# Pinned places for joins, weight loads, transposes and modulation pieces, and another prologue, in a hybrid DeltaNet and RWKV-7 block

## The chip, the core and the metric

The kernel runs on one core of a Trainium2 chip. The metric is the device time of one execution in microseconds (us); lower is better. The engines are TensorE (PE, with its weight loads shown apart as PEld), VectorE (DVE), ScalarE (ACT), GpSimd (POOL) and SyncE (SP), which here only issues DMAs. Each engine works through its own instructions in a fixed order; it waits where an operand or a buffer isn't ready, and everything behind the waiting instruction waits too.

## What is computed

One decoder block on 512 tokens of width 1024, in float32. A conditioning vector `c` gives six vectors of modulation; two token mixers run beside each other on one input projection and are merged by gates; a gated convolutional feed-forward follows.

```python
cond = jax.nn.silu(c)
mod = cond @ w_ada[i] + b_ada[i]
shift1, scale1, gate1, shift2, scale2, gate2 = jnp.split(mod[:, None, :], 6, axis=-1)
h = rms_norm(x, norm1_w[i]) * (1.0 + scale1) + shift1
p = h @ w_in[i]
qkv_a, z_a, b_a, a_a, p_b, gl_a, gl_b = split_cols(p, IN_SIZES)
y_a = gated_deltanet(qkv_a, z_a, b_a, a_a, conv_gdn[i], a_log[i], dt_bias[i], onorm_gdn[i])
y_b = rwkv7_time_mix(p_b, mu_rwkv[i], w0[i], w2[i], a0[i], a2[i], g2[i], k_k[i], k_a[i], ...)
merged = sigmoid(gl_a) * (y_a @ w_branch_gdn[i]) + sigmoid(gl_b) * (y_b @ w_branch_rwkv[i])
x = x + gate1 * (merged @ w_out[i])
h = rms_norm(x, norm2_w[i]) * (1.0 + scale2) + shift2
x = x + gate2 * conv_glu(h, w_ffn_in[i], conv_ffn[i], w_ffn_out[i])
return rms_norm(x, norm_f_w)
```

Both mixers have 8 heads of width 64 and are computed in chunks of 64 tokens. In each chunk a unit lower triangular 64x64 matrix is inverted for each head (the reference's `triangular_solve`, and its counterpart for RWKV-7).

## The kernel before

**Layout and products.** Channels lie on the 128 partitions and the 512 tokens along the free axis. A product is one output tile of 128 channels: for each of 8 blocks of 128 inputs `mm3` issues three matmuls (high part of the weight by high part of the input, high by low, low by high: L186, L189, L190), which together give float32 accuracy. One full product is 24 matmuls of 128x128x512. `weights` brings a weight tile: SP loads it into `raw` (two buffers, 512 KB), ACT casts it to `whi` (L145), DVE forms the difference `wlo` (L148).

**Queue of products.** Products wait in the list `queue`; the generator `stream` issues them a triple at a time, `fill(n)` takes n triples, `need(label)` runs until a product is done, `insert` puts products in front. `weights` is called for the product now running and the next one. So the rest of the program is written between calls of `fill`, which mix products with the mixers' small matmuls. A scheduler then gives every engine its order; an edge of the class `after` ("place") only orders two instructions of one engine and makes nothing wait.

**Order of the stages.** In the prologue the square sum of `x` is taken over channels (squares on ACT, L352, adds on DVE, L354, a matmul by ones, L356). `c` arrives broadcast to 128 partitions; its SiLU is the first work of ACT (L94). `first_tiles` then computes seven products at once, block by block (`first_h`: modulation of a block, then its normalized input `hh`, `hl`). The remaining products of the input projection stand in this order: queries of the delta rule, two low-rank tiles (LO1, LO2), `z` (Z0 to Z3, stored to DRAM in `zsc`), delta-rule values (GV0 to GV3), RWKV keys and receptances (RK, RR), values (RV), gates of the first branch (GA0 to GA7), between which the eight branch products `bg` are inserted, and gates of the second (GB). Then come branch (`br`), output (`o`) and feed-forward (`fi`, `fo`) products, from about 490 us to the end.

**Solve and joins.** `solve` inverts 32x32 diagonal blocks. It stores them to DRAM (`lsc`, four DMAs, L560), loads them regrouped by block into `lt` (L563), transposes and masks (`ti`, DVE L564, POOL L565), and makes 30 pairs of DVE steps of growing width (L571, L573). After its `yield` the joins combine the blocks: four groups of 32 tiny matmuls (L594, L604), with a copy on ACT (L599) between two groups. It runs once for the delta rule (`g`), and once for RWKV-7 (`r`).

**Modulation pieces.** 32 column blocks of `w_ada`, each in two halves, make 64 pieces. `ada_half` loads a piece (`wada`, one buffer, 256 KB) and reduces it against `cond` on DVE (L209). They are attached to products by `late`.

**Transposes.** `to_natural` turns a tensor from channels to tokens in four blocks: four transposes on PE (L616) and four copies out of PSUM (L619) each. It is applied to `rv_`, `bh` and `kh`, after the `bg` products.

Of the kernel before, what the change touches and what calls it, by code (L numbers as in the profile page):

```python
# [55 lines left out]
def body(ctx, tc, io, out, tap=lambda name, ap: None):  # L56
# [121 lines left out]
    last = {"step": None, "hold": False, "gate": None, "norm": None}  # L178
# [4 lines left out]
    def mm3(p, w, j, x, start, stop):  # L183
        hi, lo = (a[j] for a in w)
        xh, xl = x
        i = pe.matmul(p, hi, xh, start=start, stop=False)  # L186
        if last["hold"]:
            tc.add_manual_dep(i.ins, last["step"].ins.name, after, reason="place")
        pe.matmul(p, hi, xl, start=False, stop=False)  # L189
        pe.matmul(p, lo, xh, start=False, stop=stop)  # L190
        return i
# [13 lines left out]
    def ada_half(j, u):  # L205
        w = wp.tile([128, T], F32, name="wada", tag="wada")
        part = slice(T * u, T * u + T)
        sp.dma_start(w, io["w_ada"][j][:, part])
        i = dve.tensor_tensor_reduce(out=w, in0=w, in1=cond[:, part], scale=1.0,  # L209
                                 scalar=half[:, j:j + 1] if u else col("b_ada", j), op0=ALU.mult, op1=ALU.add,  # L210
                                 accum_out=(mod if u else half)[:, j:j + 1])
        if last["gate"] is not None:
            tc.add_manual_dep(i.ins, last["gate"].ins.name, after, reason="place")
            last["gate"] = None

    first_half = []
# [13 lines left out]
    def stream():  # L230
        while queue:
# [113 lines left out]

    table(SILU)
    fn(cond, cond, AF.Silu)
    table(EXP)
    total = tmp("rs")
    for k in range(KT):  # L350
        sq = total if k == 0 else tmp("sq")
        act.activation(sq, xT(k), AF.Square)  # L352
# [3 lines left out]
    pe.matmul(p, one, total, start=True, stop=True)  # L356
# [4 lines left out]
    first_ps = [mm(), mm(), pa(), pa(), pc(), pc(), pc()]  # L361
# [4 lines left out]
    first_w = []  # L366

    def load_ada(k):
        for j in ((0,), (1, 2))[k] if k < 2 else (k + 1,):
            if j < KT:  # L370
                w = slot((2, 3, 8, 9, 12)[j]) if j < 5 else slot2((0, 2, 1)[j - 5])
                first_w.append(w)
                sp.dma_start(w[:, 0:D], io["w_ada"][8 + j])
                sp.dma_start(w[:, D:2 * D], io["w_ada"][j])

    def first_h(k):
# [110 lines left out]
    last["gate"] = dve.scalar_tensor_tensor(gl, s3, -1.0, bc(nea), op0=ALU.mult, op1=ALU.mult)  # L487
# [65 lines left out]
    def solve(sv, name, work):  # L553
# [9 lines left out]
        sp.dma_start(lt, lsc)  # L563
# [22 lines left out]
        yield  # L586
        for h in range(2):
# [636 lines left out]
```

## Time and profile before

| | |
|---|---|
| median of 3 runs | 934.77 us (933.60 to 935.44) |
| profiled execution | 937.31 us |
| its span, first to last instruction | 935.6 us |
| mean granted TensorE clock | 0.983 |
| modulation pieces, DVE (L209) | 64 reductions, first at 91.9 us, last at 480.4 us |
| solve `g`: stores of `lsc` issued, first step, joins | 121.5, 143.1, about 205 to 212 us |
| solve `r`: stores of `lsc` issued, load of `lt` issued | 314.3, 328.9 us |
| transposes of `rv_`, `bh`, `kh` on PE | up to 381 us |

The profile is one execution; idle time stands in square brackets in front of an instruction, with what ended it. The granted clock is TensorE's, 1 for full speed.

### The profile page before, as it was taken

The numbers are of one execution on the slowest core, as the hardware profiler recorded it, in microseconds if no ns is written. First come the engines' busy times: TensorE is split into PE (matmuls) and PEld (weight loads), VectorE is DVE, ScalarE is ACT, GpSimd is POOL, SyncE is SP. The second block draws the span as 40 slices with busy tenths as digits, with TensorE's granted clock in tenths as the row PEclk, the third lists the DMA queues.
The fourth block names the chain that finished last, engine by engine and source line by source line (L and its number), as shares of the span: only waits on it lengthen the run. The fifth ranks groups of instructions, "written<-read, shape, count | busy, mean of one in ns | idle before, by whom it ended". The sixth has DMA issues, their size and how long they took to land.

```text
span 935.6 us, 13853 instructions
## 1 busy us (share of the span) xinstructions
PE 876.3 (94%) x5459; PEld 687.7 (74%) x5459; DVE 533.3 (57%) x858; ACT 419.2 (45%) x680; POOL 95.2 (10%) x91
## 2 busy tenths in 40 slices
PE   2999999999989978899999999999999999999996
PEld 1886577677656666677668888888888888888885
DVE  5987859824696786255476537564445445332233
ACT  5367543734554747632465335343333333333231
POOL 1000300000352300001230120000000000010112
PEclk9999999997999989899999999999999999999998
DMA  9841245363323367644546542322322322533322
GB/s 332 283 149 67 91 105 185 109 166 112 103 82 113 69 213 267 162 147 148 183 158 202 171 141 84 111 91 92 109 92 90 105 99 90 179 98 100 107 80 91
DMA packets 81119, 125.72 MB, mean 134 GB/s; under 512 B 26045, under 2 KB 42813, under 8 KB 80990
## 3 DMA queue, kind: packets, MB, share of 16 engines
q1 hardware_dynamic: 81054, 124.83, 42.2%
q8 instruction: 43, 0.70, 0.3%
q14 instruction: 22, 0.18, 0.1%
HBM read 110.13 MB, written 14.16 MB: 133 GB/s over the span
## 4 chain that ended last, share of the span: by engine, by line
PE 69%; DVE 10%; DMA 6%; ACT 6%; issue 6%; POOL 2%; SPq 0%; DVEq 0%; POOLq 0%; ACTq 0%
PE ps_mm L186 19%; PE ps_mm L189 18%; PE ps_mm L190 18%; DMA wada<-in_w_ada 4%; DVE wlo L148 2%; PE ps_pc L181 2%; DVE wada L209 1%; ACT tmp_rs L94 1%; PE ps_pc L186 1%; PE ps_pc L189 1%; PE ps_pc L190 1%; ACT slot L619 1%; PE ps_pa L186 1%; PE ps_pa L189 1%; PE ps_pa L190 1%
## 5 line engine op out<-in xcount | busy, mean ns | idle before, releaser
L186 PE MATMUL ps_mm<-hh,whi 128*128 128x512 f32 (+1 forms) x642 | 264.2, 412 | 9.8 <-ACT hh L308 3.4
L148 DVE TENSOR_TENSOR wlo<-raw,whi 128x1024 fp32r<-128x1024 f32 (+2 forms) x140 | 161.2, 1152 | 176.2 <-ACT whi L145 170.6
L190 PE MATMUL ps_mm<-hh,wlo 128*128 128x512 f32 (+1 forms) x642 | 255.0, 399 | 1.3 <-DVE wlo L148 1.3
L189 PE MATMUL ps_mm<-hl,whi 128*128 128x512 f32 (+1 forms) x642 | 253.8, 396 | 0.0
L145 ACT CAST whi<-raw 128x1024 fp32r<-128x1024 f32 (+2 forms) x140 | 137.1, 979 | 259.7 <-PE ps_mm L189 198.4
L186 PEld LDWEIGHTS ps_mm<-hh,whi 128*128 128x128 f32 x642 | 121.5, 190 | 46.8 <-issue 8.5
L190 PEld LDWEIGHTS ps_mm<-hh,wlo 128*128 128x128 f32 x642 | 121.6, 189 | 31.6 <-issue 3.4
L189 PEld LDWEIGHTS ps_mm<-hl,whi 128*128 128x128 f32 x642 | 122.1, 190 | 26.7 <-issue 4.0
L186 PE MATMUL ps_mm<-slot,whi 128*128 128x512 f32 (+1 forms) x226 | 85.7, 379 | 4.7 <-ACT tmp_sp L94 4.7
L190 PE MATMUL ps_mm<-slot,wlo 128*128 128x512 f32 (+1 forms) x226 | 85.1, 376 | 0.0
L189 PE MATMUL ps_mm<-slotd,whi 128*128 128x512 f32 (+1 forms) x168 | 62.4, 371 | 0.0
L186 PEld LDWEIGHTS ps_mm<-slot,whi 128*128 128x128 f32 x226 | 43.2, 191 | 12.6 <-ACT tmp_sp L94 4.9
L190 PEld LDWEIGHTS ps_mm<-slot,wlo 128*128 128x128 f32 x226 | 43.1, 191 | 7.7
L189 PE MATMUL ps_mm<-slot,whi 128*128 128x512 f32 (+1 forms) x122 | 45.3, 372 | 0.0
L186 PE MATMUL ps_mm<-slotd,whi 128*128 128x512 f32 (+1 forms) x96 | 36.4, 379 | 0.0
L190 PE MATMUL ps_mm<-slotd,wlo 128*128 128x512 f32 (+1 forms) x96 | 36.1, 376 | 0.0
L209 DVE CUSTOM_DVE_ANT_0 wada<-wada,cond,cols 128x512 f32<-128x512 f32 x32 | 25.6, 800 | 18.3 <-DMA wada<-in_w_ada 18.2
L189 PEld LDWEIGHTS ps_mm<-slotd,whi 128*128 128x128 f32 x168 | 31.6, 188 | 5.7
L1099 DVE TENSOR_TENSOR tmp_sg<-tmp_acc,ps_mm 128x512 f32<-128x512 f32 x20 | 13.8, 688 | 36.0 <-PE ps_mm L190 35.8
L209 DVE CUSTOM_DVE_ANT_0 wada<-wada,cond,half 128x512 f32<-128x512 f32 x32 | 24.9, 779 | 14.6 <-DMA wada<-in_w_ada 14.4
L398 DVE SCALAR_TENSOR_TENSOR tmp_acc<-ps_mm,cols,tmp_acc 128x511 f32<-128x511 f32 (+2 forms) x44 | 32.8, 746 | 0.7
L1032 POOL COPY tmp_rs<-tmp_sq 128x512 f32<-128x512 f32 x2 | 2.1, 1064 | 304.0 <-ACT tmp_sq L1029 304.0
(270 smaller groups left out, 1262.5 us busy)
## 6 DMA issues: line engine op xcount, KB each, us to landing
raw<-in_w_in SPq DMA_DIRECT2D x40, 512.0 KB, 4.1
raw<-in_w_fi SPq DMA_DIRECT2D x37, 512.0 KB, 3.5
wada<-in_w_ada SPq DMA_DIRECT2D x64, 256.0 KB, 2.7
raw<-in_w_fo SPq DMA_DIRECT2D x16, 512.0 KB, 3.6
slot<-in_w_ada SPq DMA_DIRECT2D x10, 512.0 KB, 8.5
slot<-in_xT SPq DMA_DIRECT2D x16, 256.0 KB, 4.6
raw<-in_w_out SPq DMA_DIRECT2D x8, 512.0 KB, 3.4
raw<-in_w_in SPq DMA_DIRECT2D x8, 448.0 KB, 4.5
```

The source lines that it names most:

```text
L94: i = act.activation(*a, **k)
L145: i = act.copy(hi, src)
L148: j = eng.tensor_tensor(lo, src, hi.bitcast(F32), op=ALU.subtract)
L181: last["step"] = pe.matmul(*a, **k)
L186: i = pe.matmul(p, hi, xh, start=start, stop=False)
L189: pe.matmul(p, hi, xl, start=False, stop=False)
L190: pe.matmul(p, lo, xh, start=False, stop=stop)
L209: i = dve.tensor_tensor_reduce(out=w, in0=w, in1=cond[:, part], scale=1.0, scalar=half[:, j:j + 1] if u else col("b_ada", j), op0=ALU.mult ...
L398: dve.scalar_tensor_tensor(acc[:, i:], p[:, :T - i], w[:, taps - 1 - i:taps - i], acc[:, i:], op0=ALU.mult, op1=ALU.add)
L619: (act.copy if e == c or quiet else dve.tensor_copy)(place(e, 2 * b + c), p[hs(c), :, e, :])
L1032: pool.tensor_copy(sums[0], sq)
L1099: dve.tensor_tensor(t, accs[j], p, op=ALU.mult)
```

## The change

The computation and its results stay the same; only places and one layout change.

Prologue: `c` comes as one row (4 KB in two loads), is broadcast by a matmul with ones into PSUM, and SiLU reads it there, behind the sixth square. `cols` and the first half of the first modulation weights are loaded between tiles of `x`. 34 small matmuls by ones are added on PE ahead of and behind the sum matmul. The first scale `A1` is made on DVE.

```diff
-        if k == 3:
-            sp.dma_start(cond, io["c"])
-    sp.dma_start(cols, io["cols"])
+        if k == 2:
+            sp.dma_start(cols, io["cols"])
+        if k == KT - 2:
+            sp.dma_start(first_w[0][:, 0:D], io["w_ada"][8])
...
-    fn(cond, cond, AF.Silu)
-    table(EXP)
+    i = work(8, None)
+    for u in range(2):
+        m = pe.matmul(first_ps[u], one[0:1], crow[u], start=True, stop=True)
...
+    i = work(16, i)
...
+        if k == KT - 2:
+            for u in range(2):
+                c = fn(cond[:, T * u:T * u + T], first_ps[u], AF.Silu)
+                tc.add_manual_dep(c.ins, q.ins.name, after, reason="place")
+            table(EXP)
...
+    work(10, m)
```

Weight loads: each raw load that is made after a `solve` began stands on SP behind that solve's load of `lt`.

```diff
-        sp.dma_start(raw[:, :n], src)
+        i = sp.dma_start(raw[:, :n], src)
+        if last["load"] is not None:
+            tc.add_manual_dep(i.ins, last["load"].ins.name, after, reason="place")
...
-        sp.dma_start(lt, lsc)
+        last["load"] = sp.dma_start(lt, lsc)
```

SP's order at the first solve. `zsc` is a store of a finished Z product, `lsc_g` the stores of the blocks, `slot<-lsc_g` the load of `lt`, `raw` a weight tile. Before:

```order
L156 DMA raw<-in_w_in 128x1024 x6
L208 DMA wada<-in_w_ada 128x512 x2
L156 DMA raw<-in_w_in 128x1024
L208 DMA wada<-in_w_ada 128x512 x3
L409 DMA zsc<-tmp_sp 128x512
L560 DMA lsc_g<-slotd_851 32x32x32 x4
L409 DMA zsc<-tmp_sp 128x512 x2
L156 DMA raw<-in_w_in 128x1024
L563 DMA slot_957<-lsc_g 128x1024
```

Now:

```order
L161 DMA raw<-in_w_in 128x1024 x5
L454 DMA zsc<-tmp_sp 128x512
L605 DMA lsc_g<-slotd_891 32x32x32 x4
L454 DMA zsc<-tmp_sp 128x512
L608 DMA slot_997<-lsc_g 128x1024
L161 DMA raw<-in_w_in 128x1024 x4
L454 DMA zsc<-tmp_sp 128x512
```

In both, one raw load of a single product stands further ahead. So eight weight tiles of single products were issued before the stores of `lsc` (to Z3), and six now (to Z1); Z2's comes after the load of `lt`, as does all that follows from it on ACT and DVE. DVE's order now, from the last work on the blocks (L716) on; L609 makes `ti`, L616 and L618 are the solve's steps, and the first `wlo` is Z2's:

```order
L716 TENSOR_TENSOR slotd_499<-slotd_499,slot_672 128x512 x4
L609 TENSOR_SCALAR slot_997<-slot_997 128x1024
L616 TENSOR_TENSOR pr<-slot_997 128x30
L618 TENSOR_TENSOR slot_997<-slot_997,pr 128x30
L616 TENSOR_TENSOR pr<-slot_997 128x58
L618 TENSOR_TENSOR slot_997<-slot_997,pr 128x29x2
L616 TENSOR_TENSOR pr<-slot_997 128x84
L153 TENSOR_TENSOR wlo<-raw,whi 128x1024
```

Before, Z2's `wlo` stood ahead of the solve.

Joins: every group is ordered behind the last product matmul issued before it, and the following products behind the group (`last["join"]`, `last["mm"]`).

```diff
+        def join(*a):
+            last["join"] = pe.matmul(*a, start=True, stop=True)
+            tc.add_manual_dep(last["join"].ins, behind[0].ins.name, after, reason="place")
...
             fill(2)
+            behind[0] = last["mm"]
```

PE's order at the joins of the first solve. Before, `slot_957` being the solved blocks, with the products of RK and RR around (of which two stand here):

```order
L189 MATMUL ps_mm<-hl_119,whi 128x512
L190 MATMUL ps_mm<-hh_111,wlo 128x512
L594 MATMUL ps_pa<-slot_957,slotd_851 32x32 x31
L604 MATMUL ps_pa<-slotd_851,tmp_sg 32x32
L594 MATMUL ps_pa<-slot_957,slotd_851 32x32 x32
L604 MATMUL ps_pa<-slotd_851,tmp_sg 32x32 x63
```

Now:

```order
L635 MATMUL ps_pa<-slot_997,slotd_891 32x32 x32
L193 MATMUL ps_mm<-hh_109,whi 128x512
L198 MATMUL ps_mm<-hl_117,whi 128x512
L199 MATMUL ps_mm<-hh_109,wlo 128x512
L193 MATMUL ps_mm<-hh_110,whi 128x512
L198 MATMUL ps_mm<-hl_118,whi 128x512
L199 MATMUL ps_mm<-hh_110,wlo 128x512
L635 MATMUL ps_pa<-slotd_891,tmp_sg 32x32 x32
```

One clump of about 127 became four groups of 32, with six product matmuls between two of them.

Modulation pieces: `ada_half` is split into a load and a reduction, each ordered behind the product's matmul at a fixed step (`at_step`), the reduction four triples behind the load. Their places: `late=2` on RK, RR, on GB and on the two last gates, 1 on GA, on one `br` and on seven `o` products, and 1 on feed-forward products, which take the last 16.

```diff
+                    if todo and at % gap == 0 and at // gap < todo:
+                        loaded = ada_load(*ada_rest.pop(0))
                     mm3(p, q["w"], k, it["xs"][at], at == 0, at == it["n"] - 1)
+                    if loaded and at % gap == min(gap - 1, 4):
+                        ada_half(*loaded)
+                        loaded = None
```

Transposes: `bh` and `kh` are turned together by `to_natural_2`, in place, with four triples of products after each of the four blocks, directly after `bg` is inserted and not behind it. The `z` tiles: two are loaded before the RWKV matrices are built, two behind the load of `lt` of the second solve.

```diff
+    to_natural_2(bh, kh)
+    kb = [kh, bh]
     need(("bg", KT - 1))
...
-    kb = [ct4(slot(2)), bh]
-    to_natural(bh, lambda e, c: kb[e][hs(e), :, c * C:(c + 1) * C], True)
-    to_natural(kh, lambda e, c: kb[e][hs(1 - e), :, c * C:(c + 1) * C], True)
+    fill(6)
```

ACT's order after the second solve's load, now: L94 on `tmp_sg` is the SiLU of a `z` tile, L150 on `slot_2839` the high part of the gated result that `bg` reads, L676 a copy of the moved transposes, and the cast to `whi` that of GA2's weights; the first row stands directly behind the SiLU table load, and a sixteenth copy ahead of that.

```order
L94 ACTIVATE tmp_sg<-tmp_sg 128x512 x2
L676 COPY slot_1397<-ps_pa 64x4x64
L676 COPY slot_1879<-ps_pa 64x4x64
L150 CAST slot_2839<-tmp_rs 128x512 x2
L676 COPY slot_1879<-ps_pa 64x4x64
L676 COPY slot_1397<-ps_pa 64x4x64 x2
L676 COPY slot_1879<-ps_pa 64x4x64 x2
L676 COPY slot_1397<-ps_pa 64x4x64 x2
L676 COPY slot_1879<-ps_pa 64x4x64 x2
L676 COPY slot_1397<-ps_pa 64x4x64 x2
L676 COPY slot_1879<-ps_pa 64x4x64 x2
L150 CAST whi<-raw 128x1024
L94 ACTIVATE tmp_sg<-tmp_sg 128x512 x2
```

Before, no copies of transposes stood here, and the cast of GA2's weights (the only one of 128x1024) stood ahead of the table load:

```order
L145 CAST whi<-raw 128x1024
L94 ACTIVATE tmp_rs<-tmp_rs 128x512
L859 ACTIVATE tmp_sq<-slotd_459 128x512 x2
L94 ACTIVATE tmp_rs<-ps_pa,kc 128x512
...
L88 ACT_TABLE_LOAD
L94 ACTIVATE tmp_sg<-tmp_sg 128x512 x2
L145 CAST whi<-raw 128x512
L145 CAST slot_2753<-tmp_rs 128x512 x2
```

More of the change, by code (lines that the diff above doesn't have):

```diff
@@ L186, in mm3 @@
         i = pe.matmul(p, hi, xh, start=start, stop=False)
+        if last["join"] is not None:
+            tc.add_manual_dep(i.ins, last["join"].ins.name, after, reason="place")
         if last["hold"]:
@@ L203, in ada, with at_step, ada_load, ada_half @@
             tc.add_manual_dep(i.ins, last["norm"].ins.name, after, reason="place")
-    def ada_half(j, u):
+    def at_step(i):
+        if last["mm"] is not None:
+            tc.add_manual_dep(i.ins, last["mm"].ins.name, after, reason="place")
+    def ada_load(j, u):
         w = wp.tile([128, T], F32, name="wada", tag="wada")
[L207 to L216, printed above, removed]
+        at_step(sp.dma_start(w, io["w_ada"][j][:, T * u:T * u + T]))
+        return j, u, w
+    def ada_half(j, u, w):
+        at_step(dve.tensor_tensor_reduce(out=w, in0=w, in1=cond[:, T * u:T * u + T], scale=1.0,
+                                         scalar=half[:, j:j + 1] if u else col("b_ada", j), op0=ALU.mult, op1=ALU.add,
+                                         accum_out=(mod if u else half)[:, j:j + 1]))
     ada_rest = [(j, u) for j in range(16, 48) for u in range(2)]
@@ L236, in stream @@
                     nx["begin"] = None
-            for _ in range(min(it["late"], len(ada_rest))):
-                ada_half(*ada_rest.pop(0))
+            todo, loaded = min(it["late"], len(ada_rest)), None
+            gap = it["n"] // todo if todo else 0
             for i, q in enumerate(it["pieces"]):
@@ L346, in body, with work @@
     table(SILU)
-    fn(cond, cond, AF.Silu)
-    table(EXP)
+    first_ps = [mm(), mm(), pa(), pa(), pc(), pc(), pc()]
+    def work(n, i):
+        for _ in range(n):
+            j = pe.matmul(first_ps[6][:, 0:128], one, one, start=True, stop=True)
+            if i is not None:
+                tc.add_manual_dep(j.ins, i.ins.name, after, reason="place")
+            i = j
+        return i
+    i = work(8, None)
+    for u in range(2):
+        m = pe.matmul(first_ps[u], one[0:1], crow[u], start=True, stop=True)
+        tc.add_manual_dep(m.ins, i.ins.name, after, reason="place")
+        i = m
+    i = work(16, i)
     total = tmp("rs")
+    q = None
     for k in range(KT):
+        if k == KT - 2:
+            for u in range(2):
+                c = fn(cond[:, T * u:T * u + T], first_ps[u], AF.Silu)
+                tc.add_manual_dep(c.ins, q.ins.name, after, reason="place")
+            table(EXP)
         sq = total if k == 0 else tmp("sq")
-        act.activation(sq, xT(k), AF.Square)
+        q = act.activation(sq, xT(k), AF.Square)
+        if k == KT - 2:
+            tc.add_manual_dep(q.ins, order["load"].ins.name, after, reason="place")
         if k > 0:
@@ L821, in body @@
     tap("go", go)
+    zts = [tmp("sg"), tmp("sg")]
+    for ct in range(2):
+        sp.dma_start(zts[ct], zsc[ct])
     for _ in prep:
@@ L869, in body @@
     for ct in range(4):
-        zt, sg = tmp("sg"), tmp("rs")
-        sp.dma_start(zt, zsc[ct])
+        if ct > 1:
+            zts.append(tmp("sg"))
+            i = sp.dma_start(zts[ct], zsc[ct])
+            tc.add_manual_dep(i.ins, last["load"].ins.name, after, reason="place")
+        zt, sg = zts[ct], tmp("rs")
         fn(zt, zt, AF.Silu)
@@ L1105, in body @@
     for i in range(7, 2 * NF):
-        queue.append(product(("fi", i), io["w_fi"][i], h2, (glu_up if i % 2 else glu_gate)(i // 2)))
+        queue.append(product(("fi", i), io["w_fi"][i], h2, (glu_up if i % 2 else glu_gate)(i // 2), late=1))
     prefetch()
```

66 lines of the change are left out of this document (44 added, 22 removed).

## The prediction

> **What bounds the kernel now.** I read the page first, then the chain of waits, then busy time by stretch, and then the timeline where a stretch has TensorE idle or at a low clock. The page's engine row and its chain row:
>
> ```profile
> PE 876.3 (94%) x5459; PEld 687.7 (74%) x5459; DVE 533.3 (57%) x858; ACT 419.2 (45%) x680; POOL 95.2 (10%) x91
> ...
> PE 69%; DVE 10%; DMA 6%; ACT 6%; issue 6%; POOL 2%; SPq 0%; DVEq 0%; POOLq 0%; ACTq 0%
> ```
>
> TensorE (PE) is busy 94% of the 935.6 us span, so the change can win only what PE loses: idle time, and time at a lowered clock. The stretches show where. Their columns are the stretch, its length, busy time and count on PE, PE's weight loads, DVE, ACT and POOL, then PE's granted clock, DMA share and GB/s.
>
> ```profile
> 0.00:20.40 20.40, 2.06 (x3) 0.52 (x3) 8.83 (x13) 11.77 (x16) 2.78 (x13) 1.00 0.93 327
> 20.40:73.30 52.90, 52.90 (x249) 43.49 (x249) 48.83 (x71) 26.39 (x40) 0.52 (x1) 1.00 0.64 221
> 73.30:123.70 50.40, 45.96 (x264) 31.08 (x262) 41.65 (x81) 31.78 (x59) 9.80 (x11) 0.97 0.21 67
> 123.70:165.00 41.30, 37.64 (x167) 30.02 (x165) 30.09 (x62) 15.21 (x25) 1.27 (x1) 1.00 0.53 161
> 200.00:222.00 22.00, 20.66 (x326) 15.79 (x325) 6.09 (x10) 9.45 (x15) 0.00 (x0) 0.77 0.36 121
> 246.00:297.00 51.00, 45.26 (x458) 31.25 (x459) 43.36 (x65) 25.97 (x52) 26.35 (x23) 1.00 0.32 95
> 324.00:343.00 19.00, 14.30 (x58) 11.51 (x57) 15.07 (x34) 10.44 (x17) 1.27 (x1) 0.82 0.48 163
> 363.40:381.50 18.10, 14.86 (x78) 10.06 (x75) 7.50 (x20) 17.50 (x42) 0.00 (x0) 1.00 0.92 226
> 381.50:395.00 13.50, 11.62 (x305) 9.86 (x303) 1.92 (x2) 8.43 (x18) 0.00 (x0) 0.86 0.58 197
> 395.00:490.00 95.00, 93.51 (x835) 65.79 (x833) 56.00 (x100) 40.01 (x70) 16.83 (x14) 0.98 0.49 156
> 575.00:930.00 355.00, 351.69 (x1613) 293.25 (x1611) 152.29 (x177) 121.13 (x158) 15.10 (x12) 1.00 0.32 101
> ```
>
> From 575 us on PE idles 3.3 us in 355, and DVE is busy for only 43% of it. So the 16 modulation pieces that now come there are hidden, and I cost them at nothing; if DVE were full there, they would cost 16 x 0.8 = 13 us. All the rest is decided before 400 us.
>
> **The change, part by part.** The sum is made against the profiled execution, 937.31 us.
>
> *Prologue.*
>
> ```profile
> 9.10 1.06 ACT L94 ACTIVATE cond<-cond 128x1024 f32<-128x1024 f32 x1 [1.06 <-DMA cond<-in_c]
> ...
> 12.13 3.08 DVE L354 TENSOR_TENSOR tmp_rs<-tmp_rs,tmp_sq 128x512 f32<-128x512 f32 x4 [3.36 <-ACT tmp_sq L352]
> ...
> 15.36 2.04 PE L356 MATMUL ps_pa<-tmp_rs,one 128*128 128x512 f32 x2 [15.36 <-DVE tmp_rs L354]
> 20.38 1.22 PE L186 MATMUL ps_mm<-hh,whi 128*128 128x512 f32 x2 [2.98 <-ACT hh L308]
> ```
>
> SiLU over the broadcast `c` waits for 512 KB and holds up the squares behind it; DVE's adds wait 3.36 us for these squares, and the sum matmul starts at 15.36. In the changed order `c` is 4 KB, and SiLU stands behind the sixth square. The wait (1.06), most of DVE's 3.36 and half of the sum matmul's 2.04 (PE has by then run its added 26 small matmuls) go: 4 to 5 us at the first product, and about 2.5 more if the first products run at full clock. What is late next is DVE, busy 48.83 of the following 52.90 us: it has about 4 us of slack to follow in. I take -4, between -1.5 (only the wait and part of the adds) and -6.
>
> *Pieces taken out of the first convolutions and the delta-rule matrices.* DVE's busy time of the reductions alone, from 123.7 to 165:
>
> ```profile
> 123.70:165.00 41.30, 4.53 (x12) 1.00 0.53 161
> ```
>
> That is six reductions, each with the read of its sum, 0.75 us apiece. Five of them leave DVE's order between 73 and 124 us, 3.8 us with what they wait for their loads on top. PE idles 50.40 - 45.96 = 4.4 us there. I take -2.5, between -4.4 and 0.
>
> *Load of the triangle ahead (first solve).* SP issues in order. The order above shows that the load of `lt` now stands ahead of the raw weights of product Z2, which in the kernel before were issued long before it.
>
> ```profile
> 121.49 3.20 SPq L560 DMA_DIRECT2D lsc_g<-slotd  x4
> ...
> lsc_g<-slotd SPq DMA_DIRECT2D x4, 128.0 KB, 3.8
> slot<-lsc_g SPq DMA_DIRECT2D x1, 512.0 KB, 4.6
> raw<-in_w_in SPq DMA_DIRECT2D x40, 512.0 KB, 4.1
> ...
> 126.06 0.39 PE L186 MATMUL ps_mm<-hh,whi 128*128 128x512 f32 x1
> ...
> 126.74 0.39 PE L186 MATMUL ps_mm<-hh,whi 128*128 128x512 f32 x1
> ...
> 139.42 1.23 DVE L148 TENSOR_TENSOR wlo<-raw,whi 128x1024 fp32r<-128x1024 f32 x1 [9.20 <-ACT whi L145]
> 140.56 1.10 DVE L564 TENSOR_SCALAR slot<-slot 128x1024 f32<-128x1024 f32 x1
> 143.10 0.19 DVE L571 TENSOR_TENSOR pr<-slot 128x30 f32<-128x30 f32 x1 [1.43 <-POOL slot L565]
> ```
>
> In the times of before: the stores end at 124.7 and land 3.8 later, 128.5; `lt` lands 4.6 later, 133.1, its raw weights about the same time. Both ACT's cast and, on DVE, the difference `wlo` come behind that: DVE has the 1.10 of `ti`, POOL's 1.43, five short steps (the first 0.19, about 1.2 with the gaps) and `wlo` 1.23, which makes 138. PE wants Z2's first weights at 126.74. It can run two matmuls before it needs `wlo`, so it idles about 10.5 us and comes back at a low clock. A wait of 4.70 us shows what that costs:
>
> ```profile
> 334.74 0.79 PE L186 MATMUL ps_mm<-slot,whi 128*128 128x512 f32 x1 [4.70 <-ACT tmp_sp L94]
> ...
> 340.02 0.46 PE L186 MATMUL ps_mm<-slot,whi 128*128 128x512 f32 x1
> ```
>
> Twelve matmuls in 5.28 us, against three in 0.68 us from 126.06 (0.227 each): 2.5 lost. Of the 41.30 - 37.64 = 3.7 us that PE idles here now, most goes. Sum 10.5 + 2.5 - 3.7, so I take +9, between +5 (`wlo` early, all of the old idle gone) and +13 (no old idle gone). The solve itself then ends sooner, which nobody waits for: its joins come only at 207 us.
>
> *Pinned joins.*
>
> ```profile
> 207.47 0.21 PE L604 MATMUL ps_pa<-slotd,tmp_sg 32*32 32x32 f32 x1 [0.67 <-ACT tmp_sg L599]
> ...
> 209.35 2.91 PE L604 MATMUL ps_pa<-slotd,tmp_sg 32*32 32x32 f32 x126 [0.68 <-ACT tmp_sg L599]
> ```
>
> Two waits of 0.67 us per solve go, since six matmuls now stand between two blocks (6 x 0.227 = 1.4 us). The clock in that stretch is 0.77 over 22 us: 0.23 x 22 / 0.5 = 10 us at half speed, at most 5 us lost. I take -5 for the first solve (-1.4 to -6.4). For the second, the clock of 0.86 and then 0.98 gives 0.14 x 13.5 + 0.02 x 95 = 3.8 us lost at most besides the waits: -4 (-1.9 to -5.7).
>
> *Modulation at fixed steps, recurrence.*
>
> ```profile
> DVE wada L209 <- DMA wada<-in_w_ada: 32.5, 25, 3.7
> ```
>
> DVE stands 32.5 us behind these loads in all; a load four matmul triples ahead (4 x 3 x 0.227 = 2.7 us) leaves little of it. Only where PE follows DVE closely does it count: in the delta-rule recurrence, where PE idles 51.00 - 45.26 = 5.7 us and DVE is busy 43.36, and about half of the reductions leave. I take -4 (-5.7 to 0). In the second recurrence PE idles 1.5 us in 95: nothing.
>
> *Transposes of `bh` and `kh` moved.* From 363.4 to 381.5 PE's 78 instructions are 41 full matmuls (9.3 us), 35 transposes and 2 small ones; 18.10 - 9.3 = 8.8 us are the transposes' and their waits. They go from here: -8.5 (-10 to -5). What they cost where they now stand is in the next term.
>
> *Weights of GA2 (the third gate product of the first branch).* Their raw load stands behind `lt` of the second solve, their cast on ACT behind a table, two SiLUs, two casts and 16 copies of transposes, as the order shows.
>
> ```profile
> 320.65 0.80 PE L186 MATMUL ps_mm<-hh,whi 128*128 128x512 f32 x1
> ...
> 324.01 1.28 ACT L88 ACT_TABLE_LOAD   x1
> 325.31 1.15 ACT L94 ACTIVATE tmp_sg<-tmp_sg 128x512 f32<-128x512 f32 x2
> ...
> 326.88 1.14 ACT L145 CAST slot<-tmp_rs 128x512 fp32r<-128x512 f32 x2
> ...
> L145 ACT CAST whi<-raw 128x1024 fp32r<-128x1024 f32 (+2 forms) x140 | 137.1, 979 | 259.7 <-PE ps_mm L189 198.4
> L619 ACT COPY slot<-ps_pa x72: 364/368/373, 121.3 to 383.5; 64x256 f32<-64x256 f32 x72
> ```
>
> ACT: 324.0 + 1.28 + 1.15 + 1.14 + 16 x 0.368 + 0.98 = 334.4, then `wlo` at 335.7. PE runs nine matmuls and 16 transposes from 320.65 (at (14.86 - 9.3) / 35 = 0.16 each) and is there at 325: 10 us of idle, 2.5 at low clock, and two more blocks of transposes (16 x 0.16 = 2.5). Before, 4.70 + 2.5 was lost in the same place, and that goes. Net +7.5, between +4 (copies overlapped) and +13 (the old loss stays).
>
> *Sum:* -4 - 2.5 + 9 - 5 - 4 - 4 - 8.5 + 7.5 = -11.5, so 925.8. The timed median lies 2.5 below the profiled execution (934.77 against 937.31): **923**. Its own ends, from the terms taken together, are 914 and 931.
>
> **Rivals.**
> - *The weights come in time (A).* If the tail of either queue is shorter than I think, each wait halves: Z2 at +2 and GA2 at 0 make the sum -26, so 909. For it speaks that raw loads have two buffers and that DMA has room (share 0.21 before 124 us); against it, that both waits stand in a fixed order on SP and ACT.
> - *Slower: the solve stands ahead of the weights on DVE (B).* The solve's two kinds of steps, from 165 to 200 us, on DVE:
>
> ```profile
> 165.00:200.00 35.00, 5.15 (x16) 1.00 0.54 149
> ...
> 165.00:200.00 35.00, 5.35 (x16) 1.00 0.54 149
> ```
>
> These 10.5 us now come before 165. There 4.5 us of reductions leave, so 6 us more stand ahead of a `wlo` for which PE waits; the same at the second solve, where DVE is already busy 15.07 of 19.00. With GA2's wait at its upper end: 15 + 13 + 6 - 28 = +6, so 941. It decides where the waits for weights together cost over 30 us. Against it: the order puts a `wlo` between the steps from the fifth on.
> - *The reliefs give nothing (C).* DVE paces the first 73 us (48.83 of 52.90) and the recurrence (43.36 of 51); a DVE that is still full swallows the prologue's 4, the 2.5 and the 4. Sum -1: 934, within 0.2%.
> - *The joins did not lower the clock (D).* Their longest gap is 0.68 us. If the clock falls for other reasons, only the gaps go: 1.4 and 1.3 in place of 5 and 4, sum -5.2, so 930.
>
> [...] The trace disagrees: the clock is 0.77 in that stretch, though PE was busy 20.66 of 22.00 us. [...] So D is a small chance.
>
> **How the numbers follow.** Forecast 0.45, A 0.17, B 0.14, C 0.14, D 0.10. The time is the forecast's, 923. The range reaches down to near A and up to near B: 906 to 940. A measurement of this kernel can tell 0.2% from no change, 1.9 us. Faster: 0.45 + 0.17 + 0.10 + 0.03 of C = 0.75; same 0.09 of C; slower 0.14 + 0.02 of C = 0.16.
>
> **What would show it.** Right: the first product before 17 us; PE idle some 10 us at Z2, waiting for `wlo` or `whi`, and again at GA2 behind the SiLU table; joins without waits and a clock near 1 around them; no stretch with 35 transposes after bg. Wrong: no PE wait above 5 us at either place (A), `wlo` late at several products in a row (B), the same 50 us per recurrence (C), a clock below 0.9 at the spread joins (D). The forecast fails most easily on the two waits, 23 us of idle that no row of before contains.

## The result, and the profile after

The changed kernel takes 943.19 us (median of 8 executions, 942.12 to 946.15), the kernel before 935.50 in the same comparison (8 executions): a ratio of 1.0084, 95% interval 1.0070 to 1.0098. It is slower by 7.7 us; the forecast was 923, range 906 to 940. The profiled executions differ by less: 942.24 against 937.31, so 4.9 us. The stage table below explains those 4.9; the 2.8 us between them and the medians can't be assigned to a stage. One execution among those below, 1160.16 us of f4's seven, ran in a slower state, and the ratios leave it out.

The page after, engines and chain:

```profile
PE 889.8 (95%) x5531; PEld 697.1 (74%) x5531; DVE 541.4 (58%) x859; ACT 417.6 (44%) x680; POOL 94.6 (10%) x91
...
PE 67%; DVE 11%; ACT 9%; DMA 7%; issue 4%; POOL 1%; SPq 1%; DVEq 0%; ACTq 0%; POOLq 0%
```

TensorE's own share of the chain of waits falls from 69 to 67%, ACT's rises from 6 to 9%: PE waits more for weights. To compare stages I counted the 3207 product matmuls of each trace and cut both spans at the start of the n-th. Busy time by stretch (matmuls 300 to 408, 408 to 576, 576 to 624, 624 to 753, 753 to 840, 840 to 978, 1200 to 1400), with the columns of the prediction's rows. Before:

```profile
123.99:153.12 29.13, 25.47 (x110) 19.88 (x108) 17.96 (x36) 9.66 (x18) 1.27 (x1) 1.00 0.58 172
153.12:200.08 46.96, 45.41 (x195) 34.14 (x195) 35.90 (x83) 26.45 (x43) 0.00 (x0) 1.00 0.50 146
200.08:223.96 23.88, 22.54 (x333) 17.35 (x332) 6.09 (x10) 9.47 (x16) 0.00 (x0) 0.79 0.34 114
223.96:297.28 73.32, 67.58 (x635) 46.56 (x633) 54.40 (x85) 38.71 (x73) 28.20 (x26) 1.00 0.33 98
297.28:342.86 45.58, 38.81 (x370) 28.93 (x366) 32.69 (x69) 29.48 (x62) 8.74 (x5) 0.93 0.41 120
342.86:395.12 52.26, 45.92 (x463) 35.29 (x462) 28.01 (x69) 35.96 (x76) 0.00 (x0) 0.96 0.77 229
489.86:535.20 45.34, 45.34 (x202) 37.54 (x200) 28.96 (x41) 21.21 (x30) 2.83 (x2) 1.00 0.56 182
```

The same stretches, by number of matmul, after:

```profile
115.80:155.10 39.30, 29.31 (x119) 22.86 (x117) 29.95 (x64) 12.46 (x24) 2.63 (x3) 0.83 0.46 140
155.10:207.60 52.50, 48.30 (x257) 36.24 (x257) 23.10 (x41) 27.79 (x45) 0.00 (x0) 0.97 0.46 131
207.60:222.70 15.10, 15.10 (x243) 12.16 (x241) 6.64 (x12) 6.78 (x12) 0.00 (x0) 1.00 0.41 111
222.70:297.30 74.60, 69.43 (x664) 47.41 (x662) 50.82 (x78) 40.18 (x76) 28.04 (x26) 1.00 0.26 78
297.30:348.20 50.90, 42.52 (x392) 31.29 (x389) 32.59 (x75) 40.05 (x93) 8.15 (x5) 0.90 0.33 90
348.20:397.30 49.10, 45.66 (x473) 35.64 (x471) 20.84 (x49) 25.08 (x45) 0.00 (x0) 0.90 0.70 219
491.40:539.50 48.10, 46.34 (x202) 37.16 (x201) 35.14 (x55) 20.99 (x30) 2.85 (x3) 1.00 0.68 219
```

| product matmuls | what the change does there | forecast, us | measured, us |
|---|---|---|---|
| start to 168 | prologue | -4 | -3.9 |
| 168 to 300 | pieces out of the first convolutions (but see p1) | -2.5 | -4.3 |
| 300 to 408 | triangle loaded ahead of Z2's weights | +9 | +10.2 |
| 408 to 576 | solve ends sooner | 0 | **+5.5** |
| 576 to 624 | first joins | -5 | -8.7 |
| 624 to 753 | first recurrence, fixed steps | -4 | +1.3 |
| 753 to 840 | GA2's weights | +7.5 | +5.3 |
| 840 to 978 | transposes gone (-8.5), second joins (-4) | -12.5 | **-3.1** |
| 978 to 1200 | second recurrence | 0 | -0.6 |
| 1200 to 1400 | pieces at fixed steps in the last gates, branch and first `o` products | 0 | **+2.7** |
| 1400 to the end | the rest | 0 | +0.6 |
| sum | | -11.5 | +4.9 |

The waits that were foreseen are there. TensorE's timeline after, at Z2 (matmul 312), at RK's last tile (528), at GA2 (792) and at GA4 (936); the bracket is the idle time before a row and who ended it:

```profile
128.48 0.79 PE L193 MATMUL ps_mm<-hh,whi 128*128 128x512 f32 x1 [8.34 <-ACT whi L150]
...
131.02 0.80 PE L199 MATMUL ps_mm<-hh,wlo 128*128 128x512 f32 x1 [1.32 <-DVE wlo L153]
...
192.96 0.50 PE L193 MATMUL ps_mm<-hh,whi 128*128 128x512 f32 x1 [1.71 <-ACT whi L150]
...
194.22 0.80 PE L199 MATMUL ps_mm<-hh,wlo 128*128 128x512 f32 x1 [0.53 <-DVE wlo L153]
...
330.96 0.80 PE L193 MATMUL ps_mm<-hh,whi 128*128 128x512 f32 x1 [3.83 <-ACT whi L150]
...
375.83 0.79 PE L193 MATMUL ps_mm<-hh,whi 128*128 128x512 f32 x1 [2.91 <-ACT whi L150]
```

8.34 + 1.32 us at Z2, against 10.5 forecast; 3.83 at GA2, with 2.73 more at 326.47 for the copies behind the transposes, against 10. ACT's timeline after names what the two casts waited for:

```profile
127.38 1.04 ACT L150 CAST whi<-raw 128x1024 fp32r<-128x1024 f32 x1 [5.75 <-DMA raw<-in_w_in]
...
325.03 1.78 ACT L676 COPY slot<-ps_pa 64x256 f32<-64x256 f32 x5
...
327.16 2.79 ACT L676 COPY slot<-ps_pa 64x256 f32<-64x256 f32 x8 [0.35 <-PE ps_pa L670]
...
329.86 1.04 ACT L150 CAST whi<-raw 128x1024 fp32r<-128x1024 f32 x1
...
374.73 1.05 ACT L150 CAST whi<-raw 128x1024 fp32r<-128x1024 f32 x1 [0.89 <-DMA raw<-in_w_in]
```

At Z2 it is the raw load behind `lt`; at GA2 the copies of the moved transposes right ahead of the cast. The late weights at 375 stand on SP behind reloads of the second solve's blocks:

```profile
365.93 1.52 SPq L628 DMA_DIRECT2D slotd<-usc_r  x3
...
370.28 0.39 SPq L161 DMA_DIRECT2D raw<-in_w_in  x1
```

### The profile page after: what moved, and what is told of

It is laid out like the page before. It is cut to its first block, busy times and chain, and to the rows that moved or that the text cites. A ratio compares the mean times of both kernels' runs of the same rounds, so it can differ in the third digit from the quotient of the medians.

```text
span 940.5 us, 13981 instructions
## 1 busy us (share of the span) xinstructions
PE 889.8 (95%) x5531; PEld 697.1 (74%) x5531; DVE 541.4 (58%) x859; ACT 417.6 (44%) x680; POOL 94.6 (10%) x91
## 4 chain that ended last, share of the span: by engine, by line
PE 67%; DVE 11%; ACT 9%; DMA 7%; issue 4%; POOL 1%; SPq 1%; DVEq 0%; ACTq 0%; POOLq 0%
PE ps_mm L193 18%; PE ps_mm L199 18%; PE ps_mm L198 17%; DMA wada<-in_w_ada 5%; DVE wlo L153 3%; PE ps_pc L188 3%; ACT tmp_rs L94 2%; ACT whi L150 1%; DVE wada L225 1%; PE ps_pc L199 1%; PE ps_pc L198 1%; PE ps_pc L370 1%; PE ps_pc L193 1%; PE ps_pa L198 1%; PE ps_pa L199 1%
## 5 line engine op out<-in xcount | busy, mean ns | idle before, releaser
L150 ACT CAST whi<-raw 128x1024 fp32r<-128x1024 f32 (+2 forms) x140 | 136.8, 979 | 278.6 <-PE ps_mm L198 211.6
L198 PEld LDWEIGHTS ps_mm<-hl,whi 128*128 128x128 f32 x642 | 122.9, 192 | 27.4 <-issue 4.0
L225 DVE CUSTOM_DVE_ANT_0 wada<-wada,cond,half 128x512 f32<-128x512 f32 x32 | 28.5, 891 | 11.2 <-DMA wada<-in_w_ada 11.0
L94 ACT ACTIVATE tmp_acc<-tmp_acc 128x512 f32<-128x512 f32 x22 | 13.9, 633 | 41.8 <-DVE tmp_acc L443 41.5
```

The source lines that it names most:

```text
L94: i = act.activation(*a, **k)
L150: i = act.copy(hi, src)
L225: at_step(dve.tensor_tensor_reduce(out=w, in0=w, in1=cond[:, T * u:T * u + T], scale=1.0, scalar=half[:, j:j + 1] if u else col("b_ada", j ...
```

## The experiments

Every number is a median, with its ratio to the kernel before on the same chip. "Late" and "early" by stage are read as above, from one profiled execution each, which can lie several us from the median; "the end" is the last product matmul.

### One part undone, and prologue and joins alone

```diff
 a1: weights()
-        if last["load"] is not None:
-            tc.add_manual_dep(i.ins, last["load"].ins.name, after, reason="place")
 a2: transposes of bh and kh back behind bg
-    to_natural_2(bh, kh)
-    fill(6)
+    to_natural(bh, lambda e, c: kb[e][hs(e), :, c * C:(c + 1) * C], True)
+    to_natural(kh, lambda e, c: kb[e][hs(1 - e), :, c * C:(c + 1) * C], True)
 a3: ada_half, its places and its order as before
 b1: kernel before + new prologue + pinned joins
```

> The changed kernel without the edge that puts raw weight loads behind the load of lt. Theory P (the pinned loads cost the time): the wait at Z2 (8.3 and 1.3 us) and the low clock behind it go, and most of the wait at GA2: 12 to 17 us less than the changed kernel's 943, so 926 to 931. Rival R (the waits are set by the order on ACT and DVE, and weights would be late anyway): under 4 us less, 939 or more.

**940.50, 1.0058 (1.0032 to 1.0085).** The wait at Z2 is gone: matmuls 300 to 456 take 42.2 us instead of 52.4. Only a quarter of these 10 us arrives at the end. 480 to 552 takes 27.0 us as in the changed kernel (before: 23.1), and the second joins stay late. At GA2 783 to 792 falls to 2.7 us, but 753 to 840 as a whole stays at 51.3 (50.9 in the changed kernel). The profiled execution, 945.50, is its longest.

> The changed kernel with the transposes of bh and kh where they stood before, one tensor after the other behind bg. If the 16 copies on ACT make GA2's weights late (my term): the wait there falls from about 8 to 2 us, but the 9 us of transposes come back ahead of the joins: 940 to 944. If the joins' new wait for weights (2.9 us at 375.8, and the low clock) comes from the loads of the solved blocks, which the transposes used to cover: that wait goes too, and the whole is 936 to 940. If moving the transposes gained what I forecast (8.5 us): 948 or more.

**941.89, 1.0061 (1.0039 to 1.0084).** 783 to 792, in front of GA2, takes 5.5 us, not 9.9, and 753 to 840 takes 45.6, as before. TensorE's timeline of a2 there:

```profile
325.53 0.50 PE L193 MATMUL ps_mm<-hh,whi 128*128 128x512 f32 x1 [1.94 <-ACT whi L150]
...
330.58 0.79 PE L199 MATMUL ps_mm<-hh,wlo 128*128 128x512 f32 x1 [4.32 <-DVE wlo L153]
```

The wait for weights only changes its place: without the copies the cast is early, and `wlo` is late on DVE. At 942 to 960, among the second joins, 17.3 us pass instead of 9.9: the gain is given back there.

> The changed kernel with the modulation pieces placed as before (3 for a gate of the first branch, 4 for the second, 2 for an output product, the scheduler free to move them). Theory P2 (fixed steps cost what was lost between 408 and 576 and from 1200 to 1400 product matmuls, 5.5 and 2.7 us, and gained 4 between 192 and 300): 938 to 941. Rival: the losses there are the solve's loads and the order on ACT, and only the gain goes: 945 to 948.

**941.13, 1.0054 (1.0033 to 1.0074).** 1200 to 1400 takes 45.5 us, as before (45.3): the 2.7 us there belong to the pieces' new places and steps, which a3 undoes together. Both waits for weights remain.

> The kernel before with two parts of the change alone: the prologue and the pinned joins. If the gains that the trace shows at these places (3.9 us at the first products, 8.7 at the first joins) are the parts' own and stay: 920 to 924 with a gain at the second joins of 1 to 4 as well. If they were made by the other parts (the clock at the joins, or a DVE freed of modulation pieces): 928 to 933.

**929.27, 0.9929 (0.9906 to 0.9952).** Faster than both kernels. Its profiled execution, 932.97, is its longest, so its stages understate it: 8.9 us early at matmul 753, 4.1 at the end.

A line that goes with the pinned joins in all these kernels is `need(T_RK + 2)`: it runs the products up to the third of RK before the joins are written, and those of the first solve start at matmul 576 (before, at 562).

No undone part alone returns the 7.7 us, and the parts share places: at the second joins each relief runs into something else. So I added the other parts one by one to b1.

### One part added to b1

```diff
 c1: b1 + modulation at fixed steps
 c2: b1 + to_natural_2 in its new place + z tiles loaded ahead
 c3: b1 + the order of raw loads behind the load of lt
 c4: b1 + z tiles + that order only from the third weight tile on; z stores behind lt
+        if last["load"] is not None:
+            last["free"] -= 1
+            if last["free"] < 0:
+                tc.add_manual_dep(i.ins, last["load"].ins.name, after, reason="place")
```

> Prologue and pinned joins (929) plus the modulation pieces at fixed steps. Theory P2 (the fixed steps cost at RK and RR, where a wlo stands behind a reduction, and in the output and first feed-forward products): 4 us lost between product matmuls 480 and 552 and 3 to 4 between 1200 and 1400, 1 to 3 gained before 456: 933 to 937. Rival (the losses at these places belong to the pinned loads): 926 to 930.

**937.60, 1.0018 (0.9992 to 1.0045):** 8.3 us above b1. just above what I expected. It has no ordered loads, yet 480 to 552 takes 27.0 us.

> Prologue and pinned joins (929) plus the moved transposes and the z tiles loaded ahead, without the pinned weight loads. Theory W (the second joins wait for the second solve, whose loads end near 370 us; a transpose ahead of them costs nothing, one moved to bg costs): the joins start no more than 7 us earlier, and 3 to 5 us are lost at GA2 and bg to the copies: 926 to 931. Rival (the transposes' 9 us are real and their move gains them): 920 or less.

**935.20, 1.0003 (0.9985 to 1.0022):** 5.9 above b1, and above both expectations. At the second joins PE waits 4.7 and 3.9 us for the reloads of the solved blocks, in the longest of its executions (940.16). 753 to 840 takes 51.8 us (b1 44.2), with no load ordered.

> Prologue and pinned joins (929) plus the pinned weight loads alone. Theory P: waits of 8 to 10 us at Z2 and 3 to 7 us at GA2, with low clock behind both; the first solve ends 8 us sooner, which its joins use by at most 3: 936 to 943. Rival R: under 3 us more, 929 to 932.

**956.00, 1.0217 (1.0202 to 1.0232):** 26.7 above b1, far above what I expected. 300 to 336 takes 22.4 us (b1 9.6), 783 to 792 takes 12.2 (b1 2.5), the longest of all kernels, and the second joins start at 393.9. Against b1, 300 to 408 loses 8.5 us, 753 to 840 7.9 and 480 to 552 4.4. No copy was moved here, so the ordered loads alone make the loss at GA2, as the moved transposes (with the z tiles) do in c2.

> Prologue and pinned joins (929) plus the load of lt ahead in another way: the stores of z stand behind it, the first two weight tiles after each solve's start don't, later ones do; and z is loaded ahead as in the change. Theory P: lt is issued some 6 us sooner at both solves with no wait at Z2 or GA2, and both joins, which wait for the solved blocks, follow: 921 to 926. Rival (an earlier lt is worth nothing): 928 to 931.

**942.07, 1.0074 (1.0056 to 1.0092):** the triangle comes early, 300 to 408 loses only 2.9 us against b1 and GA2 nothing (783 to 792 takes 2.5 us), and it is still 12.8 above b1, above both expectations (its profiled execution, 938.60, is its shortest and b1's the longest, so its stages show 5.6 of these). This speaks against my step that only the waits for weights cost something. 480 to 552 takes 26.6 us here, too.

One at a time, steps, transposes and order cost 8.3, 5.9 and 26.7 us over b1, 40.9 in sum; all at once they cost 13.9. They meet at the same places and don't add up.

### The prologue alone, and the second solve

```diff
 p1: kernel before + new prologue
 d2: b1, half of the transposes' copies on VectorE
-    to_natural(bh, ..., True)
-    to_natural(kh, ..., True)
+    to_natural(bh, ...)
+    to_natural(kh, ...)
 e1: b1, second lt ahead
+        if last["load"] is not None and n == T:
+            tc.add_manual_dep(i.ins, last["load"].ins.name, after, reason="place")
 e2: e1 + d2
```

> The kernel before with the other prologue alone. If prologue and joins each keep what they gain: 931 to 933 (3.7 us less at the first seven products, and the same 3.7 at the end). If the second joins wait for the second solve whatever happened before (and the solve starts 3.7 us sooner too), the same; if something later swallows it: 934 to 936.

**935.68, 1.0012 (1.0002 to 1.0022).** 3.3 us early after the first products and 8.2 early at matmul 912, but 4.7 early at 978, behind the second joins, 2.4 at 1200, 1.8 at the end, and nothing in the median. The prologue does more than it should: matmuls 168 to 300 with the wait in them, before and in p1:

```profile
61.26:123.99 62.73, 58.29 (x343) 41.21 (x342) 53.18 (x96) 40.65 (x73) 9.80 (x11) 0.97 0.23 74
```

```profile
82.81 0.47 PE L186 MATMUL ps_mm<-hh,whi 128*128 128x512 f32 x1 [2.06 <-DVE tmp_acc L398]
```

```profile
58.01:116.64 58.63, 55.80 (x335) 38.90 (x334) 52.31 (x91) 38.17 (x68) 8.55 (x10) 1.00 0.22 71
```

```profile
78.21 0.50 PE L191 MATMUL ps_mm<-hh,whi 128*128 128x512 f32 x1 [0.55 <-DVE slot L435]
```

p1 leaves the modulation pieces where they were and has 4.1 of the changed kernel's 4.3 us there. Most of what it gains is lost at the second joins and in the recurrence behind them.

> Prologue and pinned joins (929) with half of the copies behind the transposes of bh and kh on VectorE instead of ScalarE. If PE's waits there are the copies' (2.1 and 1.8 us for ScalarE in the kernel with prologue and joins): 2 to 5 us less, 924 to 927. If the second joins wait for the solved blocks anyway: 928 to 931.

**925.18, 0.9904 (0.9884 to 0.9924):** the fastest kernel of the study, 18 us below the changed one. b1's windows and TensorE timeline around its second joins:

```profile
360.00:390.00 30.00, 24.86 (x340) 18.77 (x339) 5.85 (x10) 21.45 (x46) 0.00 (x0) 0.72 0.73 203
```

```profile
363.05 0.66 PE L658 MATMUL ps_pa<-cons,slot 128*128 128x128 f32 x4 [2.06 <-ACT slot L661]
```

and d2's:

```profile
350.00:380.00 30.00, 26.46 (x379) 19.80 (x378) 17.00 (x41) 21.49 (x44) 0.00 (x0) 1.00 0.83 244
```

```profile
360.06 0.66 PE L658 MATMUL ps_pa<-cons,slot 128*128 128x128 f32 x4 [1.58 <-ACT slot L661]
...
367.35 1.19 PE L624 MATMUL ps_pa<-slot,slotd 32*32 32x32 f32 x62 [0.41 <-DMA slot<-tsc_r]
```

In b1 transposes wait for ACT's copies and PE's clock is 0.72; in d2 DVE takes half of the copies, the clock is 1.00, and the joins find their blocks with 0.41 us of waiting. These are b1's longest execution and d2's shortest, 10.4 us apart where the medians are 4.1. What holds in each pair that differs in this alone is the idle time of PE at 840 to 978: 6.97 to 3.94 us here, 7.16 to 5.75 (e1, e2), 7.45 to 4.00 (f3, g1). The clock does not hold: 0.97 to 0.91 in the last pair.

> Prologue and pinned joins (929) with the load of lt ahead at the second solve alone: the last two z tiles and the weights of bg behind it, all other weights free. The load comes some 7 us sooner (now 319.3, behind z tiles that wait for buffers). Theory W (the second joins wait for that solve): up to 7 us less where the transposes let them, 923 to 929. Rival (an earlier solve puts its DMAs ahead of weights, as at the first): 931 to 936.

**933.27, 0.9980 (0.9965 to 0.9995),** slower than b1. The triangle comes earlier, but the solve's steps end 71.1 us after matmul 753 (start of the last step; b1: 70.8): its end is not set by its start here.

> Both edits of the two kernels ahead together. Theory W: the copies and the solve bound the second joins in turn, so both together gain more than the sum of each: 920 to 926. Rival: 929 or more.

**928.11, 0.9931 (0.9905 to 0.9956).** No gain over d2; ordering the load has nothing to give.

### Is it the place or the engine of the copies? Which part lengthens 480 to 552?

```diff
 f1: the changed kernel;  f2: prologue + joins + to_natural_2;  both with
-                        act.copy((x if e else y)[o, :, at], p[hs(c), :, e, :])
+                        (act.copy if e == c else dve.tensor_copy)((x if e else y)[o, :, at], p[hs(c), :, e, :])
 f3: kernel before + pinned joins
 f4: c1, but no pieces on RK and RR
-late=2 if t >= T_GB or T_RK <= t < T_RV else 1 if t >= T_GA else 0
+late=2 if t >= T_GB else 3 if t >= T_GA else 0
```

> The changed kernel with half of the copies of the moved transposes on VectorE. If ScalarE's 16 copies set GA2's wait: the wait of about 8 us there falls by 3 to 5 and the whole to 938 to 941. If the pinned raw load sets it: 942 to 945.

**939.72, 1.0044 (1.0027 to 1.0062).** GA2's wait is 4.88 us, not smaller than the change's 3.83, and 2.98 for `wlo` follow: the number came as expected, the reason did not. On DVE `wlo` now stands behind copies and the first steps of the solve. The 3.5 us come from the second joins (930 to 978 takes 19.1 us, 26.6 in the changed kernel).

> Prologue, pinned joins and moved transposes with half of their copies on VectorE. If the copies' engine is what bounds (as in the kernel with copies on VectorE and transposes in their old place, 925): 922 to 927. If the moved place takes away the cover of the second joins' wait for the solved blocks: 928 to 935.

**937.85, 1.0031 (1.0012 to 1.0049).** TensorE's timeline of f2:

```profile
370.28 0.28 PE L624 MATMUL ps_pa<-slot,slotd 32*32 32x32 f32 x2 [9.06 <-DMA slot<-tsc_r]
375.42 1.91 PE L624 MATMUL ps_pa<-slot,slotd 32*32 32x32 f32 x62 [4.85 <-DMA slot<-tsc_r]
```

13.9 us of idle at the second joins, 9.06 in one piece, and 12.7 us more than d2, which shares the copies in the old place; above both expectations. So it is the place, not the engine: in their old place the transposes stood ahead of these joins and covered the time in which the solved blocks travel through DRAM. Part of the wait is another thing: the solve itself ends later, its last step starting 76.7 us after matmul 753 (c2 74.0, b1 70.8, d2 69.7). How much is lost cover and how much a late solve was not separated.

> The kernel before with the pinned joins alone. If the joins' gain at the first solve (4 to 7 us between product matmuls 576 and 624) is kept to the end: 929 to 932. If the second joins give back what comes before them, as they did with the prologue: 933 to 936.

**931.59, 0.9955 (0.9939 to 0.9972).** The pinned joins alone. Their stretch, matmuls 576 to 624:

```profile
200.35:215.43 15.08, 15.08 (x245) 12.15 (x241) 5.30 (x9) 7.39 (x12) 0.00 (x0) 1.00 0.38 123
```

15.08 us at clock 1.00, against 23.88 at 0.79 before. It is 6.6 us early at the end, but 1.4 of these at matmul 168, ahead of any edit; the medians differ by 4.3 (935.88 before). Its neighbours are longer, 552 to 576 by 1.9 us and 624 to 753 by 1.8. Spreading the joins and starting them later (`need(T_RK + 2)`; before, the first stood at matmul 562, the bulk at 600) were not tried apart.

> Prologue, pinned joins and fixed steps, with no piece on RK and RR (three on each gate of the first branch in their place). If the loss of 4 us at 480 to 552 comes from a solve that ends sooner because the pieces left VectorE: it stays, 934 to 940. If it comes from the pieces' loads and reductions at RK and RR: it goes, 929 to 934.

**938.46, 1.0022 (1.0005 to 1.0039).** 480 to 552 still takes 26.6 us, so the pieces on RK and RR aren't its cause. Put beside the end of the first solve (start of its last DVE step, against the start of matmul 480), the readings (of one profiled execution each) fall into two groups:

| kernel | last solve step, us after matmul 480 | matmuls 480 to 552, us |
|---|---|---|
| before, b1, c2, d2, e2, f2, f3, g1, p1 | 15.2 | 23.0 to 23.1 |
| e1 | 15.4 | 23.3 |
| a1, c1 | 6.9 | 27.0 |
| f4, c4 | 5.3, 4.7 | 26.6 |
| a3, c3 | -3.9 | 27.4 |
| after, a2, f1 | -13.4 | 26.6 to 26.7 |

Three products that take 23 us when the solve ends late take 26.6 to 27.4 when it ends early, with or without ordered loads. SP's rows show what goes past what. Before:

```profile
183.62 2.39 SPq L156 DMA_DIRECT2D raw<-in_w_in  x2
...
186.59 0.33 SPq L575 DMA_DIRECT2D tsc_g<-slot  x1
...
193.53 1.67 SPq L583 DMA_DIRECT2D slotd<-usc_g  x3
```

and a1, which has no ordered loads:

```profile
172.38 0.38 SPq L618 DMA_DIRECT2D tsc_g<-slot  x1
...
179.46 2.24 SPq L626 DMA_DIRECT2D slotd<-usc_g  x3
...
185.61 0.85 SPq L161 DMA_DIRECT2D raw<-in_w_in  x2
```

The store of the solved blocks (`tsc_g`) and their reloads go out ahead of the two raw loads instead of behind them, and TensorE waits for the weights: counted from matmul 480 (171.1 us before, 165.1 in a1) the two raw loads go out 8 us later. a1's timeline:

```profile
192.16 0.50 PE L191 MATMUL ps_mm<-hh,whi 128*128 128x512 f32 x1 [1.71 <-ACT whi L150]
```

That an early end goes with the loss is shown in every kernel; that the queue on SP is the whole of it, and not also DVE and ACT around the casts, was not isolated.

### Joins and shared copies without the prologue

```diff
 g1: d2 with the old prologue
```

> The kernel before with the pinned joins and half of the copies of the old transposes on VectorE, without the prologue. If the second joins had swallowed the prologue's gain and no longer do: 928 to 930, 3 to 4 above the kernel with the prologue (925.2). If the prologue is worth nothing here either: 924 to 926.

**927.94, 0.9916 (0.9902 to 0.9929).** Against f3, which differs only in who makes the copies, 3.6 us less, and the intervals don't meet. So sharing the copies is worth 3.6 us here. d2, with the prologue too, has 925.18; its interval overlaps with this one, so 2.8 us is the prologue's likely worth there, not a sure one.

## Why the prediction was wrong

**Right.** The wait at Z2 with its cause and size (+10.2 for +9). The first joins' sign and reason: spread out they run at clock 1.00 and gain 8.7 rather than 5 in their stretch; in f3 it is 8.8, and the neighbours give back 1.9 and 1.8, which leaves 5.1. The 16 feed-forward pieces, "I cost them at nothing": they stand at matmuls 1740 to 2120, which take 86.7 us instead of 86.1.

**Near in number, not in cause.** The stretch of the pieces "taken out of the first convolutions", -4.3 for -2.5, owes them 0.2: c1 has 58.5 us there, b1 58.7, p1 58.6, and the kernels with the old prologue (before, f3, g1) 62.65 to 62.77. The 4.1 are the prologue's. Its -3.9 up to 168 is partly luck: with the same old opening f3 and g1 take 59.8 and 59.6 us, where the profiled execution before took 61.3. By matmul 300 the prologue alone (p1) is 7.4 us early against before and 5.7 to 5.8 against those two, for -4. At GA2, +5.3 for +7.5, the waits were 3.83 and 2.73 us instead of 10, and the copies are not the cause alone: c3 loses 7.9 there without them, and in a2 `wlo` is late in their place. Of -11.5 forecast, these five terms (prologue, pieces, Z2, GA2, first joins) make +5.0 and measure -1.4. They did not turn the sign.

**The step that failed most: "They go from here: -8.5", together with -4 for the second joins.** 840 to 978 gave -3.1 instead of -12.5. The time of the transposes was counted from TensorE's side only, and nothing was booked for what would be late next. In the changed kernel PE's idle time there did fall, 52.26 - 45.92 = 6.3 to 49.10 - 45.66 = 3.4 us, and 22 of 36 transposes went (the forecast let all 35 of its window go; 14 of `rv_`'s stand here now, 4 before). In their place PE waits 2.91 us for GA4's weights, which stand behind the blocks' reloads on SP, and the clock falls: 0.10 x 49 = 5 us lost instead of 0.04 x 52 = 2, so the joins' -4 did not come. The blocks themselves are in time there: the joins start at 379.27 with no wait of their own. Where the transposes are moved and loads aren't ordered, PE waits for the blocks (f2: 9.06 + 4.85; c2 likewise): they come through DRAM, and the transposes had been the work beside that. The same place takes what other parts win earlier: p1 comes with 8.2 us in hand and leaves with 4.7. My own rule, that where a stall goes one says what is late next, was not applied here. What does shorten the waits at this place, and is kept to the end, is not moving the transposes but sharing their copies (g1, d2).

**"The solve itself then ends sooner, which nobody waits for".** True of its joins, but its stores and reloads are DMAs in SP's order, and they moved ahead of weights for which PE waits. 480 to 552 costs 3.5 to 4.3 us more in each of the nine kernels whose solve ends early. 408 to 576 was +5.5 for 0, and 3.7 of it lie there. I had looked at who waits for the solve, and not at what its instructions push aside.

**"All the rest is decided before 400 us."** 1200 to 1400, at 490 to 540 us, gave +2.7. The prediction's rows jump from 490 to 575, so it read no row there. Seven modulation pieces now stand in the last gates, branch and first `o` products of this stretch, where before had none (its last at 480.4). It is lost in part in c1 (+1.5) and f4 (+2.1), which have the fixed steps, and not in b1, c2 or a3. DVE's busy time rises there from 28.96 to 35.14, and TensorE idles 48.10 - 46.34 = 1.8 us where it idled nothing. DVE's and TensorE's rows after show the pair:

```profile
512.54 0.75 DVE L225 CUSTOM_DVE_ANT_0 wada<-wada,cond,cols 128x512 f32<-128x512 f32 x1 [0.98 <-DMA wada<-in_w_ada]
```

```profile
521.68 0.50 PE L199 MATMUL ps_mm<-slot,wlo 128*128 128x512 f32 x1 [0.78 <-DVE wlo L153]
```

A reduction at a fixed step makes DVE wait for its load, and `wlo` for a later product stands behind it; from 513.2 to 521.6 DVE has no gap above 0.30 us. That these rows explain the 2.7 us is argued; that the pieces at their new places and steps cost them is shown.

**-4 in the first recurrence** came as +1.3. The pinned joins alone make it +1.8 (f3, b1), so against b1 the changed kernel has -0.5. With the steps added to b1 it was +2.9 against b1 (c1), without pieces on RK and RR -2.4 (f4). Why the sign depends on this was not tested and stays open.

**The rivals.** B (slower, 941) had the sign and nearly the number, but not the mechanism: the stretches with the two waits together stayed near the forecast (15.5 for 16.5, where B needed over 30), `wlo` was late by 1.32 us at Z2, and the loss came from reliefs that were given back or never came. C (reliefs swallowed) was closest in kind, but I had DVE swallow them before 300 us, where the prologue's were kept; what swallows them stands at the second joins, near 380. D (the joins did not lower the clock) falls with f3: the same joins, spread, at clock 1.00 instead of 0.79.

## What to carry to other kernels

A stretch of work on the critical engine that stands ahead of a rendezvous is cover for whatever arrives there: before its time is booked as a gain, find the arrival's own time, and expect earlier gains to be lost there, too (f2 took 12.7 us more than d2, a later solve included). When a side chain is made to end sooner, list its DMAs and what they overtake in a queue that issues in order (here 3.5 to 4.3 us at 480 to 552). Read a row of every stretch in which something will stand that did not stand there, and test a term in a kernel that lacks it, even where the number fits: p1 showed whose the 4.3 us were. Test parts by adding them to a good base one at a time: undoing one of several that meet at the same place showed almost nothing here (940.5 to 941.9 in all three), and the base (b1), with d2's change of engine, beat both kernels.

## What the hardware showed unexpectedly

In the changed kernel the clock also fell behind much shorter waits than the 8.34 us at Z2, which has 0.50 from 128 to 136 us behind it. A window after, behind the waits of 1.71 and 0.53 us that end at 192.96 and 194.22:

```profile
194.00:198.00 4.00, 3.78 (x10) 3.05 (x11) 1.98 (x4) 0.00 (x0) 0.00 (x0) 0.57 0.58 194
```

PE is granted 0.57 over 4 us, 1.7 us lost. In the kernel before, three times that is lost at the clump of joins and behind it: 0.61 over 210 to 212 us, 0.50 from 212 to 220 and 0.83 from 220 to 222 make 5.1 us.

At the joins the clock fell without a wait of that size: before, some 127 matmuls of 32x32 in one clump with no gap above 0.68 us went with a clock of 0.79 over 23.88 us, and the same matmuls in four groups between products ran at 1.00 over 15.10 us (f3: 1.00 over 15.08). Whether the small matmuls or the short gaps lowered the clock was not tested.
